# Broadcasting RMS-norm factors to all partitions by DMA through a scratch row instead of by TensorE, in a two-layer decoder trunk

## The chip, the cores and the metric

One of the eight cores of one Trainium2 chip. The metric is the device time of one execution in microseconds (us); a kernel's time is the median of its runs.

## The reference, cut to what matters

The reference is a decoder trunk of two layers over 256 tokens with D_MODEL = 1024, in float32. Each layer is a half-step SwiGLU FFN (1024 to 2816 and back), a token mixer with memory cross-attention beside it, and a second half-step FFN. Layer 0 mixes with an mLSTM, layer 1 with sliding-window attention. Ahead of each of these blocks, and once for the 256 memory tokens, stands an RMS norm:

```python
def rms_norm(x, g):
    xf = x.astype(jnp.float32)
    y = xf * lax.rsqrt(jnp.mean(xf * xf, axis=-1, keepdims=True) + EPS)
    return (y * g.astype(jnp.float32)).astype(x.dtype)
def swiglu(x, w_in, w_out):
    gate, up = jnp.split(x @ w_in, 2, axis=-1)
    return (jax.nn.silu(gate) * up) @ w_out
...
x = x + 0.5 * swiglu(rms_norm(x, ffn1_norm_g[i]), ffn1_w_in[i], ffn1_w_out[i])
hn = rms_norm(x, mix_norm_g[i])
...
x = x + 0.5 * swiglu(rms_norm(x, ffn2_norm_g[i]), ffn2_w_in[i], ffn2_w_out[i])
```

There are seven such norms: one of the memory tokens, and six of x (three per layer). The factor `rsqrt(...)` is one number per token.

## The kernel before, in words

**Layout.** Activations are kept transposed: 128 features on the partitions, 256 tokens (T) along the free axis, eight such chunks. A projection of the kind "columns" has a weight tile as TensorE's stationary operand and activations as the moving one, 128x256 per matmul; a projection of the kind "rows" has the activations stationary and 256 weight columns moving.

**Precision.** Each float32 weight tile (128 x 4 x 256) arrives by a DMA on SyncE's queue (`wtile`, L216-219) and is split by `split` (L206-214) into a high half, cast by ScalarE (L211, tile `wh`), and a rest, subtracted by VectorE (L212, tile `wl`). A product is three matmuls (`mm3`, L224-228): high by high on L225, L226 and L227 for the cross terms. There are eight buffers for each half, and five for the raw tiles.

**Norms.** The norm is not applied to x. `Norm.put` (L269-279) multiplies a finished chunk of x by the gain and splits it into `xh` and `xl`, which the next block's matmuls use at once; the squares are summed over the chunks into `acc`. The factor per token is applied to what the matmuls give. `Norm.chain` (L293-310) makes it. Two float32 matmuls (L296, recorded on the helper's line L231) with 128 tokens of `acc` as stationary operand and a column of ones as moving one give the sum over the 128 partitions, one column per half of the tokens; `rsqrt_cols` (L248-251) makes the factors `rc` (128 tokens x 2 halves) on VectorE (L250) and POOL (L251). `rc` has tokens on partitions, which is what "rows" projections need. "Columns" projections need the factor along the free axis, the same on every partition. So `bcast_rows` (L253-255) has two more float32 matmuls, with a column of `rc`, broadcast to 128 columns, as stationary operand and the identity (tile `con`) as moving one; ScalarE copies their result from PSUM to `rb` (L306) and, times 0.5, to `hrb` (L309). Five norms do the second step; the memory norm and the norm before the second mixer have `rows=False` and stop at `rc`, and the norm before the first mixer makes no `hrb`.

**Users of the row.** In an FFN `hidden` (L473-483) multiplies the gate half by `rb` (VectorE, L476), applies SiLU, multiplies by the other half (L479) and splits the result (L245, L246). `hrb` is used at the FFN's end (L544). The first mixer uses `rb` on L658, L696, L697, L754 and L757.

**Order.** TensorE's and SyncE's instructions are issued in an order written out by hand: `Weave` (L61-95) steps one main program and a set of side chains, by a clock of its own that each matmul advances, and by waiting times in `LAT` (L53). `norm=7.5` is the time from the end of a block to `chain`, `norm_b=4.8` the time from there to the broadcast; `x0_b=7.5` is the same for the first norm. A consumer waits until `ready` says that the chain has run (L502, L668). The other engines' order is set by the tile framework's scheduler. A matmul's result lies in one of eight PSUM banks (`mo`, L150).

**Lines to know.** L231: all float32 helper matmuls; L236: transposes, four of 128x128 in a row; L211, L212: weight splits; L225 to L227: the weight matmuls; L183: a mask's load on POOL's queue.

Of the kernel before, what the change touches and what calls it, by code (L numbers as in the profile page):

```python
# [10 lines left out]
F32 = mybir.dt.float32  # L11
# [3 lines left out]
AF = mybir.ActivationFunctionType  # L15
ALU = mybir.AluOpType
# [3 lines left out]
P = 128  # L20
T = 256
D = 1024
# [10 lines left out]
def constants():  # L33
# [16 lines left out]

LAT = dict(pieces=1, norm=7.5, norm_b=4.8, mnorm=2.4, x0=16.0, x0_b=7.5, mkeys=7.2, cross=9.5, cross_s=1.5,  # L53
           cross_m=3.7, cross_p=8.7, cross_o=3.0, gates=20.0, scores=2.2, scores_m=8.4, num=6.9, num_r=7.5,
           keys=5.5, keys_d=7.2, query=9.0, head=1.5, head_m=2.5, head_p=9.3, head_o=4.0)

# [42 lines left out]
def tile_trunk(ctx: ExitStack, tc: tile.TileContext, a, out):  # L99
    nc = tc.nc  # L100
    seq = [0]

    def mk(pool, shape, dt, tag):
        seq[0] += 1
        return pool.tile(shape, dt, tag=tag, name=f"{tag}_{seq[0]}")

    def pool(name, bufs, **kw):
        return ctx.enter_context(tc.tile_pool(name=name, bufs=bufs, **kw))
# [13 lines left out]
    sp = pool("sp", 2)  # L122
# [8 lines left out]
    def act(*args, **kw):  # L131
        ins = nc.scalar.activation(*args, **kw)  # L132
        if args[2] not in (AF.Copy, AF.Square):
            tabled[0] = ins
# [12 lines left out]
    def col():  # L147
        return mk(cp, [P, 16], F32, "col")

    def mo():  # L150
        return mk(pb8, [P, 512], F32, "bank")
# [15 lines left out]
    ident = con[:, C_ID:C_ID + P]  # L167
    maskd = con[:, C_MASK:C_MASK + T]
    ones = mk(cst, [P, 1], F32, "ones")
# [33 lines left out]
    pieces = [1]  # L203
# [26 lines left out]
    def mmf(ps, lhsT, rhs, n, start=True, stop=True):  # L230
        nc.tensor.matmul(ps, lhsT, rhs, start=start, stop=stop, skip_group_check=True)  # L231
        wv.now += max(0.213, n * 0.00182)
# [15 lines left out]
    def rsqrt_cols(dst, src, n, scale):  # L248
        c = col()
        nc.vector.tensor_scalar(c[:, :n], src, scale, EPS, op0=ALU.mult, op1=ALU.add)  # L250
        nc.gpsimd.tensor_tensor(out=dst, in0=c[:, :n], in1=mhalf[:, :n], op=ALU.pow)  # L251

    def bcast_rows(ps, cols):  # L253
        for h in range(2):
            mmf(ps[:, h * P:(h + 1) * P], cols[:, h:h + 1].to_broadcast([P, P]), ident, P)

    def pair(x):
        return x.unsqueeze(1).to_broadcast([P, 2, T])


    class Norm:
# [30 lines left out]

        def chain(self, gap=LAT['norm_b']):  # L293
            pc = mo()
            for h in range(2):
                mmf(pc[:, h:h + 1], self.acc[:, 0, h * P:(h + 1) * P], ones, 1)  # L296
            self.rc = mk(sp, [P, 2], F32, "rc")
            rsqrt_cols(self.rc, pc[:, 0:2], 2, 1.0 / D)
            if not self.rows:
                self.done = True  # L300
                return
            yield gap
            ps = mo()
            bcast_rows(ps, self.rc)
            self.rb = mk(sp, [P, T], F32, "rb")
            nc.scalar.copy(self.rb, ps[:, :T])  # L306
            if self.half:
                self.hrb = mk(sp, [P, T], F32, "hrb")
                act(self.hrb, ps[:, :T], AF.Copy, scale=0.5)  # L309
            self.done = True  # L310

        def ready(self):
# [55 lines left out]
    def head_norm(dst, src, n, hsc):  # L368

        hd = src.shape[2] // n  # L370
        sq, v, u = tmp(), col(), col()
        sqv = sq[:, :, :n * hd]
        act(sqv, src, AF.Square)
        nc.vector.tensor_reduce(out=v[:, 0:2 * n].rearrange("p (h m) -> p h m", h=2),
                                in_=sqv.rearrange("p h (m d) -> p h m d", m=n), axis=AX.X, op=ALU.add)
        for h in range(2):
            nc.vector.tensor_scalar(u[:, n * h:n * h + n], v[:, n * h:n * h + n], hsc[:, h:h + 1], EPS,
                                    op0=ALU.mult, op1=ALU.add)
        nc.gpsimd.tensor_tensor(out=u[:, 8:8 + 2 * n], in0=u[:, 0:2 * n], in1=mhalf[:, 0:2 * n], op=ALU.pow)  # L379
        for h in range(2):  # L380
            nc.vector.tensor_scalar(v[:, 8 + n * h:8 + n * h + n], u[:, 8 + n * h:8 + n * h + n],
                                    hsc[:, 2 + h:3 + h], None, op0=ALU.mult)
        tt(out=dst.rearrange("p h (m d) -> p h m d", m=n), in0=src.rearrange("p h (m d) -> p h m d", m=n),  # L383
           in1=v[:, 8:8 + 2 * n].rearrange("p (h m) -> p h m", h=2).unsqueeze(3).to_broadcast([P, 2, n, hd]),
           op=ALU.mult)
# [12 lines left out]
    x0 = Norm(G_F1)  # L398

    def memory():  # L400
# [22 lines left out]
        def keys(gi, kr):  # L423
            nc.scalar.copy(kT[gi], turn(kr))
            return
            yield

        for gi in range(2):
# [13 lines left out]
            norm.fold()  # L442
            wv.spawn(norm.chain(), LAT['mnorm'])
            gv = Group(wkv, 512, mh, ml, rows=True)
# [5 lines left out]
            for i, q in enumerate((first, gr)):  # L450
                kr = tmp()
                head_norm(kr, q.ps, 2, hsc)
                wv.spawn(keys(i, kr), LAT['mkeys'] + 1.5 * i)
        for gi in range(2):
# [7 lines left out]
            if gi == 0:  # L462
                with tc.issue_after(last[0].ins):
                    for c2 in range(4):
                        x0.put(xT[c2])
                wv.spawn(x0.chain(LAT['x0_b']), LAT['x0'])

# [41 lines left out]
    def ffn(x, w_in, w_out, nxt=None, mid=None):  # L509
# [13 lines left out]
        for c2 in range(4):  # L523
# [25 lines left out]
            else:  # L549
                nxt.put(xn)  # L550
        wv.spawn(nxt.chain(), LAT['norm'])

# [15 lines left out]
    def cross_spawn(gr, gi, layer, hsc, ys):  # L568
# [4 lines left out]
        def queries():  # L573
# [4 lines left out]
            for m in range(2):  # L578
                wv.spawn(head(m), LAT['cross_s'] + LAT['cross_m'] * m)
            return  # L580
            yield

        def head(m):
            hd, qT = gi * 2 + m, cell[0]
            hi, lo = ys.tiles(4 + gi)
            s = mo()
            for h in range(2):
                mmf(s[:, h * T:(h + 1) * T], qT[:, m, h * P:(h + 1) * P], kT[gi][:, m], T)
            sv = halves(s)
            c = col()  # L590
            nc.vector.tensor_reduce(out=c[:, 2:4], in_=sv, axis=AX.X, op=ALU.max, negate=True)  # L591
            p = unit(F32)
            for h in range(2):
                act(p[:, h], sv[:, h], AF.Exp, bias=c[:, 2 + h:3 + h], accum_out=c[:, 4 + h:5 + h])
            nc.vector.reciprocal(c[:, 6:8], c[:, 4:6])
            tt(out=p, in0=p, in1=c[:, 6:8].unsqueeze(2).to_broadcast([P, 2, T]), op=ALU.mult)
            yield LAT['cross_p']
            tps = mo()
            for mc in range(2):
                for h in range(2):  # L600
                    transpose(tps[:, mc * T + h * P:mc * T + (h + 1) * P], p[:, h, mc * P:(mc + 1) * P])
            pT = tmp()
            nc.scalar.copy(pT, halves(tps))
            yield LAT['cross_o']
            o = mo()
            for mc in range(2):
                mmf(o[:, :T], vM[:, mc, hd * P:(hd + 1) * P], pT[:, mc], T, mc == 0, mc == 1)
            split_plain(o[:, :T], hi[:, m], lo[:, m])
            ys.done.add(8 + hd)
# [417 lines left out]
```

## Time and profile before

| What | Value |
|---|---|
| median of 3 runs (lowest, highest) | 1012.1 us (1011.96, 1012.36) |
| the profiled execution | 1012.23 us, with a span of 1010.4 us |
| mean granted TensorE clock | 1.0 |
| HBM read, written | 180.32 MB, 1.05 MB |
| DMA over the span | mean 181 GB/s |

Reading it: times are us from the span's start unless marked ns. PE is TensorE's matmuls, PEld its weight loads (they overlap the matmuls), DVE VectorE, ACT ScalarE, POOL GpSimd, SP SyncE; a q behind an engine's name is its sequencer. A row of a group gives line, engine, operation, output<-inputs with shapes, count, busy time, mean ns of one, idle time before them, and what ended it. A row of waits gives engine, tile and line that waited, what it waited for, the total, the count and the longest. A row of the timeline begins with its start and its duration. A row of a stretch gives the stretch, its length, the busy time and count of each engine in it (PE, PEld, DVE, ACT, POOL), the granted clock, the share of the DMA engines, and GB/s. A row of one tile gives durations as min/median/max ns, and first and last start. A row of a DMA gives queue, count, size and the median time from issue to landing. Matmuls are pipelined: one of 128x256 lasts about 0.28 us in the records, while the next begins well before it ends, so the pace is read from starts.

### The profile page before, as it was taken

To read this page: it belongs to the slowest core of one execution; us is meant where nothing else is said; L and a number is where in the kernel's file an instruction comes from. 1 tells how busy PE (TensorE), PEld (TensorE's weight loads), DVE (VectorE), ACT (ScalarE), POOL (GpSimd) and SP (SyncE) were. 2 spreads that over 40 slices of the span, in tenths; PEclk is the share of its full clock that TensorE was granted. 3 is DMA by queue.
4 is the path that set the end of the run, shared out by engine and by line. 5 is a ranking of instruction groups with operands and counts; after the bars stand their busy time and mean duration, and the time that the engine had idled before them with its cause. 6 is when DMAs were issued, how large, how long until landed. Compare 5 with 4: busy or idle time off the path is not lost.

```text
span 1010.4 us, 20624 instructions
## 1 busy us (share of the span) xinstructions
PE 998.5 (99%) x8594; PEld 980.2 (97%) x8594; DVE 655.5 (65%) x1063; ACT 519.5 (51%) x764; POOL 35.7 (4%) x32
## 2 busy tenths in 40 slices
PE   8999999999999999999999999999999999999998
PEld 7999999999999999999999999999987899999998
DVE  6866665577856676665558666656787766666551
ACT  7754445446656554444445544544557754454440
POOL 1200000000001000000000000000121000000000
PEclk9999999999999999999999999999999999999999
DMA  9776656666644566665676666567541347666550
GB/s 308 242 245 200 192 180 185 199 183 179 184 139 133 167 210 195 200 189 170 192 206 205 189 191 201 173 197 198 182 131 66 100 131 220 198 189 185 188 170 21
DMA packets 173204, 182.70 MB, mean 181 GB/s; under 512 B 7124, under 2 KB 168328, under 8 KB 173112
## 3 DMA queue, kind: packets, MB, share of 16 engines
q1 hardware_dynamic: 171872, 179.60, 58.3%
q10 hardware_dynamic: 1016, 1.58, 0.5%
q8 instruction: 67, 1.10, 0.5%
q0 software_dynamic: 224, 0.22, 0.2%
q14 instruction: 25, 0.20, 0.1%
HBM read 180.32 MB, written 1.05 MB: 180 GB/s over the span
## 4 chain that ended last, share of the span: by engine, by line
PE 94%; DVE 3%; ACT 1%; DMA 1%; POOL 0%; issue 0%; SPq 0%; ACTq 0%
PE bank L225 30%; PE bank L226 30%; PE bank L227 30%; PE bank L231 2%; PE bank L236 1%; ACT u L132 1%; DVE wl L212 1%; DMA wr<-in_mem_w_kv_dram 1%; PE bank L961 1%; POOL col L379 0%; DVE col L930 0%; DVE u L383 0%; DVE col L591 0%; PE bank L925 0%; DVE u L946 0%
## 5 line engine op out<-in xcount | busy, mean ns | idle before, releaser
L212 DVE TENSOR_TENSOR wl<-wr,wh 128x1024 fp32r<-128x1024 f32 (+1 forms) x347 | 414.7, 1196 | 279.8 <-ACT wh L211 279.0
L211 ACT CAST wh<-wr 128x1024 fp32r<-128x1024 f32 (+1 forms) x347 | 356.8, 1031 | 393.1 <-PE bank L226 368.9
L225 PE MATMUL bank<-xh,wh 128*128 128x256 f32 x1544 | 429.1, 278 | 0.0
L226 PE MATMUL bank<-xl,wh 128*128 128x256 f32 x1544 | 426.8, 276 | 0.0
L227 PE MATMUL bank<-xh,wl 128*128 128x256 f32 x1544 | 426.8, 276 | 0.0
L226 PEld LDWEIGHTS bank<-xl,wh 128*128 128x128 f32 x1544 | 290.3, 188 | 0.1
L225 PEld LDWEIGHTS bank<-xh,wh 128*128 128x128 f32 x1544 | 290.0, 188 | 0.1
L227 PEld LDWEIGHTS bank<-xh,wl 128*128 128x128 f32 x1544 | 289.9, 188 | 0.0
L225 PE MATMUL bank<-u,wh 128*128 128x256 f32 x896 | 249.3, 278 | 0.0
L226 PE MATMUL bank<-u,wh 128*128 128x256 f32 x896 | 247.6, 276 | 0.0
L227 PE MATMUL bank<-u,wl 128*128 128x256 f32 x896 | 247.6, 276 | 0.0
L225 PEld LDWEIGHTS bank<-u,wh 128*128 128x128 f32 x896 | 168.2, 188 | 1.9 <-issue 1.7
L226 PEld LDWEIGHTS bank<-u,wh 128*128 128x128 f32 x896 | 168.4, 188 | 0.1
L227 PEld LDWEIGHTS bank<-u,wl 128*128 128x128 f32 x896 | 168.3, 188 | 0.0
L225 PE MATMUL bank<-wh,xh 128*128 128x256 f32 x208 | 59.7, 287 | 0.0
L226 PE MATMUL bank<-wl,xh 128*128 128x256 f32 x208 | 57.9, 278 | 0.0
L227 PE MATMUL bank<-wh,xl 128*128 128x256 f32 x208 | 57.9, 278 | 0.0
L476 DVE TENSOR_TENSOR t<-bank,rb 128x256 f32<-128x256 f32 x88 | 36.6, 420 | 7.3 <-PE bank L227 7.3
L225 PEld LDWEIGHTS bank<-wh,xh 128*128 128x128 f32 x208 | 39.1, 188 | 0.5 <-issue 0.3
L226 PEld LDWEIGHTS bank<-wl,xh 128*128 128x128 f32 x208 | 39.1, 188 | 0.1
L227 PEld LDWEIGHTS bank<-wh,xl 128*128 128x128 f32 x208 | 39.0, 187 | 0.0
L479 DVE TENSOR_TENSOR t<-t,bank 128x256 f32<-128x256 f32 x88 | 32.7, 412 | 1.8 <-ACT t L132 1.8
(171 smaller groups left out, 657.5 us busy)
## 6 DMA issues: line engine op xcount, KB each, us to landing
wr<-in_ffn_w_in_dram SPq DMA_DIRECT2D x176, 512.0 KB, 3.6
wr<-in_ffn_w_out_dram SPq DMA_DIRECT2D x80, 512.0 KB, 3.5
wr<-in_a_w_in_dram SPq DMA_DIRECT2D x28, 512.0 KB, 3.9
wr<-in_b_w_in_dram SPq DMA_DIRECT2D x14, 512.0 KB, 4.6
wr<-in_a_w_out_dram SPq DMA_DIRECT2D x12, 512.0 KB, 3.3
wr<-in_b_w_out_dram SPq DMA_DIRECT2D x12, 512.0 KB, 3.4
wr<-in_ffn_w_out_dram SPq DMA_DIRECT2D x16, 256.0 KB, 2.8
wr<-in_mem_w_kv_dram SPq DMA_DIRECT2D x7, 512.0 KB, 8.0
```

The lines of the kernel that those rows point to most:

```text
L132: ins = nc.scalar.activation(*args, **kw)
L211: last[0] = nc.scalar.copy(hi[:, i * n:(i + 1) * n], src[:, i * n:(i + 1) * n])
L212: tt(out=lo[:, i * n:(i + 1) * n], in0=src[:, i * n:(i + 1) * n], in1=hi[:, i * n:(i + 1) * n].bitcast(F32), op=ALU.subtract)
L225: nc.tensor.matmul(ps, wh, xh, start=start, stop=False, skip_group_check=True)
L226: nc.tensor.matmul(ps, wh, xl, start=False, stop=False, skip_group_check=True)
L227: nc.tensor.matmul(ps, wl, xh, start=False, stop=stop, skip_group_check=True)
L231: nc.tensor.matmul(ps, lhsT, rhs, start=start, stop=stop, skip_group_check=True)
L236: nc.tensor.transpose(ps, src, ident[:k, :k])
L476: tt(out=t[:, m], in0=ps[m][:, :T], in1=x.rb, op=ALU.mult)
L479: tt(out=t[:, m], in0=t[:, m], in1=ps[m][:, T:], op=ALU.mult)
L961: nc.tensor.matmul(o[es[e], cs], vr[:, i, js], pTs[e][:, src], start=i == 0, stop=i == 1, skip_group_check=True)
```

## The change

The two broadcast matmuls and the copies from PSUM go. In their place the factors `rc` are written as one row of 256 numbers to a scratch tensor in DRAM, and that row is read back to all 128 partitions; both DMAs are issued on POOL's queue, right behind the POOL operation that makes `rc`. `hrb` is now made from `rb` by VectorE. The sum over partitions has 128 columns of ones as moving operand (a broadcast of the one column), so that its result stands 128 times, and one column of it is read. `LAT` gives the chain 12.0 (11.0 for the first norm) between that point and `done`. Each of the five norms has a row of its own in the scratch tensor `rd`.

```diff
-LAT = dict(pieces=1, norm=7.5, norm_b=4.8, mnorm=2.4, x0=16.0, x0_b=7.5, mkeys=7.2, cross=9.5, cross_s=1.5,
+LAT = dict(pieces=1, norm=7.5, norm_b=12.0, mnorm=2.4, x0=16.0, x0_b=11.0, mkeys=7.2, cross=9.5, cross_s=1.5,
...
-    def bcast_rows(ps, cols):
-        for h in range(2):
-            mmf(ps[:, h * P:(h + 1) * P], cols[:, h:h + 1].to_broadcast([P, P]), ident, P)
-
     def pair(x):
         return x.unsqueeze(1).to_broadcast([P, 2, T])
+
+    turned = []
...
         def chain(self, gap=LAT['norm_b']):
             pc = mo()
             for h in range(2):
-                mmf(pc[:, h:h + 1], self.acc[:, 0, h * P:(h + 1) * P], ones, 1)
+                mmf(pc[:, h * P:(h + 1) * P], self.acc[:, 0, h * P:(h + 1) * P], ones.to_broadcast([P, P]), P)
             self.rc = mk(sp, [P, 2], F32, "rc")
-            rsqrt_cols(self.rc, pc[:, 0:2], 2, 1.0 / D)
+            rsqrt_cols(self.rc, pc[:, :T].rearrange("p (h t) -> p h t", h=2)[:, :, 0], 2, 1.0 / D)
             if not self.rows:
                 self.done = True
                 return
+
+            rd = a["rd"][len(turned)]
+            turned.append(self)
+            self.rb = mk(sp, [P, T], F32, "rb")
+            nc.gpsimd.dma_start(rd.rearrange("(h p) -> p h", p=P), self.rc)
+            nc.gpsimd.dma_start(self.rb, rd.partition_broadcast(P))
             yield gap
-            ps = mo()
-            bcast_rows(ps, self.rc)
-            self.rb = mk(sp, [P, T], F32, "rb")
-            nc.scalar.copy(self.rb, ps[:, :T])
             if self.half:
                 self.hrb = mk(sp, [P, T], F32, "hrb")
-                act(self.hrb, ps[:, :T], AF.Copy, scale=0.5)
+                nc.vector.tensor_scalar(self.hrb, self.rb, 0.5, None, op0=ALU.mult)
             self.done = True
...
+    aps["rd"] = nc.dram_tensor("rd_dram", (5, T), F32, kind="Internal").ap()
```

## The prediction

> **What bounds the kernel now.** I read the page first: span, the engines' busy shares, the chain of work that ended last, and the group of the weight splits. Then the groups of waits of TensorE, the order of time around the seven norms, and a table of stretches for the pace of the matmuls.
>
> ```profile
> span 1010.4 us, 20624 instructions
> PE 998.5 (99%) x8594; PEld 980.2 (97%) x8594; DVE 655.5 (65%) x1063; ACT 519.5 (51%) x764; POOL 35.7 (4%) x32
> PE 94%; DVE 3%; ACT 1%; DMA 1%; POOL 0%; issue 0%; SPq 0%; ACTq 0%
> L211 ACT CAST wh<-wr 128x1024 fp32r<-128x1024 f32 (+1 forms) x347 | 356.8, 1031 | 393.1 <-PE bank L226 368.9
> PE bank L231 <- ACT u L132: 1.5, 1, 1.5
> ...
> PE bank L920 <- ACT t L954: 0.2, 1, 0.2
> ```
>
> TensorE is busy all the time and 94% of the chain is matmuls. Its list of waits (here first and last of nine) has no wait on a norm factor: L231 waits for work of the attention heads only. And ScalarE, which makes the high halves of the weights, stands idle 368.9 us because TensorE has not yet freed a buffer. So the weight pipeline is full: eight split tiles, one in use. **Only what changes TensorE's own stream, or empties that pipeline, moves the end.** The compared instruction streams say what changes there: TensorE's and SyncE's order stay, but for five broadcast blocks that go and seven sum-of-squares blocks that become wider.
>
> Now the norm of the first FFN-to-mixer step on TensorE, in order of time:
>
> ```profile
> 223.69 0.28 PE L227 MATMUL bank<-xh,wl 128*128 128x256 f32 x1
> 223.81 0.50 PE L231 MATMUL bank<-ones,acc 128*128 128x1 f32 x4
> 224.17 0.36 PE L225 MATMUL bank<-xh,wh 128*128 128x256 f32 x1
> 224.37 0.28 PE L226 MATMUL bank<-xl,wh 128*128 128x256 f32 x1
> ...
> 229.79 0.28 PE L227 MATMUL bank<-xh,wl 128*128 128x256 f32 x1
> 229.91 0.61 PE L231 MATMUL bank<-con,rc 128*128 128x128 f32 x4
> 230.27 0.37 PE L225 MATMUL bank<-xh,wh 128*128 128x256 f32 x1
> 230.47 0.28 PE L226 MATMUL bank<-xl,wh 128*128 128x256 f32 x1
> ```
>
> And the pace, by stretches cut from one matmul's start to another's (the count of weight loads, less one, is the number of steps):
>
> ```profile
> 46.34:54.70 8.36, 8.36 (x72) 8.36 (x72) 5.90 (x6) 4.20 (x4) 2.31 (x2) 1.00 0.98 318
> 55.27:223.80 168.53, 168.53 (x1489) 168.53 (x1488) 108.65 (x143) 83.26 (x102) 0.00 (x0) 1.00 0.64 192
> 230.47:252.12 21.65, 21.65 (x193) 21.65 (x192) 16.11 (x27) 13.88 (x20) 1.91 (x1) 1.00 0.63 174
> 364.42:538.38 173.96, 173.96 (x1537) 173.96 (x1536) 110.74 (x141) 84.78 (x102) 0.00 (x0) 1.00 0.64 194
> 538.96:544.48 5.52, 5.52 (x48) 5.52 (x48) 4.72 (x22) 1.77 (x3) 0.70 (x1) 1.00 0.65 190
> 545.06:719.03 173.97, 173.97 (x1537) 173.97 (x1536) 111.03 (x146) 86.16 (x104) 0.00 (x0) 1.00 0.64 193
> 840.56:1006.37 165.81, 165.81 (x1465) 165.78 (x1463) 93.21 (x119) 68.92 (x80) 0.00 (x0) 1.00 0.54 166
> ```
>
> This is the part that the averages hide. **The same matmuls run at two paces.** From 545.06 on a step is 173.97 / 1535 = 113.3 ns; from 538.96, just before, it is 5.52 / 47 = 117.4 ns, and from 46.34 it is 8.36 / 71 = 117.7 ns. The granted clock is 1.00 in all, and the DMA traffic is 190 against 193 GB/s in the neighbouring pair, so neither explains it. What lies between is a block of TensorE: the pace turns slow at each one-column sum of squares and turns fast again at each broadcast block, five times of five, and then stays for up to 1536 matmuls. I take 4.4 ns as the difference.
>
> **The change part by part.** *Broadcast blocks out.* From the L227 at 229.79 to the L226 at 230.47 are 0.68 us, where two steps would be 0.23: a block costs 0.45 us. Five go: -2.25 us. Nothing late takes their place on TensorE, because nobody there waited for them.
>
> *Sum of squares, 128 columns for one.* The 128x1 block costs, from 223.69 to 224.37, the same 0.68 us. The broadcast block has the form that the new one will have.
>
> ```profile
> L231 PEld LDWEIGHTS bank<-con,rc x20: 187/190/192, 54.6 to 840.2; 128*128 128x128 f32 x20
> L231 PE MATMUL bank<-con,rc x20: 272/275/275, 54.7 to 840.3; 128*128 128x128 f32 x20
> L231 PE MATMUL bank<-ones,acc x28: 164/250/250, 24.6 to 834.1; 128*128 128x1 f32 x28
> ```
>
> Each record goes with a weight load of 190 ns, whatever its columns, so both blocks are paced by loads: seven widened blocks cost 0 to 0.01 us each, under 0.1 us together. The Trainium skill, "TensorE: Matmul & The Clock Gate", section "Back-to-back issue gap", gives a warm step of about 60 cycles up to 64 columns and 134 at 128; by it the 28 records would cost 28 x 74 cycles, an estimate of 0.9 us, and the sum would shrink by that. The two blocks of 0.68 us speak against it here.
>
> *The slow stretch.* With a one-column block it lasts until the broadcast block: 72 matmuls once, 48 in each of the other four norms. If the widened block leaves TensorE as the equally shaped broadcast block does, these 264 run at 113.3: -264 x 4.4 ns = -1.16 us. That is the choice in this forecast. For it: five of five broadcast blocks end fast. They were entered slow, the new one is entered fast; blocks that were entered fast and have four 128-column fp32 records too are the transposes before 38.88, 315.72 and 789.06:
>
> ```profile
> 39.09:45.67 6.58, 6.58 (x61) 6.58 (x59) 6.58 (x9) 5.93 (x9) 0.00 (x0) 1.00 0.90 283
> 316.40:321.16 4.76, 4.76 (x44) 4.76 (x43) 3.02 (x8) 3.42 (x5) 0.70 (x1) 1.00 0.36 110
> 789.27:791.77 2.50, 2.50 (x25) 2.50 (x23) 1.50 (x9) 2.50 (x10) 0.00 (x0) 1.00 0.00 0
> 729.94:732.53 2.59, 2.59 (x24) 2.59 (x23) 2.56 (x6) 1.74 (x2) 0.58 (x1) 1.00 0.48 130
> ```
>
> 113.4, 113.3 and 113.6 ns a step: all fast. The last row is the counterexample: after four transposes at 729.38 it is 2.59 / 22 = 117.7, but there the activations are the stationary operand and the pace was slow before. For that reason I book nothing for the memory norm and for the norm before the second mixer.
>
> *The factor by two DMAs.* Adds, in five norms, a write of 1 KB and a read of 128 rows on POOL's queue, with POOL waiting for the first before it issues the second, and a copy for the half on VectorE; it takes two copies off ScalarE. The nearest rows, on the same queue:
>
> ```profile
> u<-in_mask_dram POOLq DMA_DIRECT2D x1, 192.0 KB, 5.5
> sink<-in_b_sinks_dram POOLq DMA_DIRECT2D x1, 8.0 KB, 5.4
> posi<-in_positions_dram POOLq DMA_DIRECT2D x1, 1.0 KB, 5.7
> con<-in_con_dram SPq DMA_DIRECT2D x1, 196.0 KB, 8.4
> 49.34 1.75 POOL L251 TENSOR_TENSOR rc<-col,mhalf 128x2 f32<-128x2 f32 x1 [13.11 <-DVE col L250]
> 51.04 0.61 POOL L183 DMA_DIRECT2D u<-in_mask_dram  x1
> 53.51 1.23 DVE L212 TENSOR_TENSOR wl<-wr,wh 128x1024 fp32r<-128x1024 f32 x1 [0.95 <-ACT wh L211]
> 57.01 1.50 DVE L476 TENSOR_TENSOR t<-bank,rb 128x256 f32<-128x256 f32 x4
> ```
>
> The write has posi's 256 elements of 4 bytes, the read is a broadcast like sink: 5.7 + 5.4 = 11.1 us. In the tightest place, the first FFN, the factors are ready at 51.09, so the row lands at 62.2. VectorE's new order puts the half copy and the first two L476 ahead of the split that ran at 53.51; VectorE then stands still some 9 us, and that split ends near 62.2 + 0.4 + 0.75 + 1.23 = 64.6 rather than 54.74. Its tile is needed six full tiles later, 6 x 24 x 113.3 ns = 16.3 us, at 71.0. So 6.4 us of cover are left, and the wait costs nothing; at con's 8.4 us per DMA the split would end at 70.3, still in time. The mask load moves behind the two DMAs on POOL; the copies off ScalarE and onto VectorE lie on engines with idle time. All of this: 0 (bounds 0 to +1).
>
> *Start-up.* VectorE's order changes by one instruction near 26 us, where a split is just late.
>
> ```profile
> PEld bank L226 <- DVE wl L212: 1.3, 2, 1.1
> ```
>
> Of these two waits the second (0.2) goes, as its split moves ahead of two small operations: -0.1, bounds -0.2 to +0.2.
>
> **Sum**: -2.25 + 0.05 - 1.16 - 0.1 = -3.5 us. The profiled execution took 1012.23 us (span 1010.4 and 1.8 around it), the median of the runs is 0.13 lower: 1012.1 - 3.5 = **1008.6**. Its own range is 1007.8 to 1009.6.
>
> **The rivals.** *Slower: the slow pace stays.* If the widened block leaves TensorE as the one-column block does (all seven of those end slow), no broadcast block follows to reset it. The stretches from 55.27, 230.47, 364.42, 545.06 and 840.56 (the second ends where projections with stationary activations begin, which run slow anyway) hold 1488 + 192 + 1536 + 1536 + 1463 = 6215 loads; at 4.4 ns that is +27.3 us, less 2.25: **1037**. It decides early: one FFN alone is 1536 x 4.4 = 6.8 us and gives 1012.1 - 3.5 + 6.8 = 1015.4. For it: same stationary operand, same entry; against it: the shape, and that every block of 128 columns in this orientation ended fast. 13%.
>
> *Slower: the row comes too late.* If the two DMAs take over 17.5 us together in the first FFN (11.1 + 6.4), TensorE waits for the split, microsecond for microsecond; at 12 us each, 1008.6 + 6.5 = 1015. The Trainium skill, "SBUF — State Buffer", section "SBUF: two separate sides", speaks for this rival: descriptors of POOL's DMAs cannot be written while VectorE holds the shared port, and it tells of 620 ns becoming 3100. The mask load above, issued while VectorE split weights, landed in 5.5 us. 4%.
>
> *No difference.* The widened block ends slow, and the pace recovers by itself after some hundred matmuls, or the mixers' phases fall worse: the gain is the 2.25 us less 0.4 to 2: 1010.3 to 1012. 6%.
>
> **How the numbers follow.** Forecast 77%, slow pace 13%, late row 4%, no difference 6%. About 0.2% (2 us) is what a measurement of this kernel can tell from no change. Faster by more: the forecast and a little of the last case, 78%; within: 6%; slower: 16%. The range takes the forecast's own and the no-difference case: 1007.6 to 1012; the slower cases, 17%, are left out.
>
> **What would show it.** Right: the matmuls after each sum of squares step at 113.3 ns at once; the L231 rows with rc are gone; the widened block still takes 0.68 us between its neighbours; VectorE's half copy waits 5 to 10 us for the row, and no TensorE wait on a split follows. Wrong: a step of 117.7 ns that runs on through an FFN (then 1015 to 1037), or TensorE waiting for L212 near 65 to 75 us.

## The result and the profile after

| | before | after |
|---|---|---|
| median of the runs (lowest, highest) | 1012.13 us (1011.96, 1012.36) | 1042.73 us (1041.11, 1044.34) |
| the profiled execution, its span | 1012.23 us, 1010.4 us | 1043.04 us, 1041.0 us |

The ratio is 1.0302, 95% interval [1.0284, 1.032]: 3% slower, where 0.35% faster was forecast. First the page of the kernel after:

```profile
span 1041.0 us, 20586 instructions
PE 1024.9 (98%) x8574; PEld 1006.5 (97%) x8574; DVE 651.7 (63%) x1067; ACT 515.2 (49%) x755; POOL 41.3 (4%) x42
PE 86%; DVE 6%; DMA 2%; POOL 2%; issue 2%; ACT 2%; SPq 0%; DVEq 0%; ACTq 0%; POOLq 0%
L211 ACT CAST wh<-wr 128x1024 fp32r<-128x1024 f32 (+1 forms) x347 | 354.3, 1027 | 362.4 <-PE bank L226 338.4
```

TensorE has 20 matmul records fewer and is busy 26.4 us longer: most of the loss is *inside* its stream, and not in waits. ScalarE still stands idle 338.4 us for a buffer that TensorE has not freed, so the weight pipeline stayed full. The same in order of time, at the norm before the first mixer:

```profile
231.43 0.28 PE L227 MATMUL bank<-xh,wl 128*128 128x256 f32 x1
231.55 0.61 PE L231 MATMUL bank<-ones,acc 128*128 128x128 f32 x4
231.91 0.36 PE L225 MATMUL bank<-xh,wh 128*128 128x256 f32 x1
232.12 0.28 PE L226 MATMUL bank<-xl,wh 128*128 128x256 f32 x1
```

From 231.43 to 232.12 are 0.69 us, against 0.68 before: the widened block itself costs nothing. What it leaves behind does. These are the stretches after each of the five row norms, cut from the second matmul behind the block to the last before the next break (count of loads less one gives the steps, as in the prediction):

```profile
47.93:231.43 183.50, 183.50 (x1560) 183.50 (x1559) 113.99 (x150) 86.87 (x104) 2.57 (x4) 1.00 0.63 193
232.12:265.80 33.68, 33.68 (x289) 33.68 (x287) 18.37 (x30) 15.65 (x21) 3.45 (x4) 1.00 0.67 157
370.26:556.58 186.32, 186.32 (x1584) 186.32 (x1583) 113.08 (x146) 85.89 (x102) 2.94 (x3) 1.00 0.62 192
557.27:743.59 186.32, 186.32 (x1584) 186.32 (x1583) 115.52 (x173) 87.27 (x105) 2.02 (x3) 1.00 0.63 187
858.99:1036.83 177.84, 177.84 (x1512) 177.84 (x1511) 95.52 (x124) 70.05 (x80) 2.98 (x3) 1.00 0.52 165
```

186.32 / 1582 = 117.8 ns a step, in all five, at a granted clock of 1.00: **the slow pace of the prediction now lasts through every FFN.** Before, 6215 of these steps ran at 113.3 ns; at 4.44 ns each that is +27.6 us.

The second loss is in the first mixer. Waits of the kernel after (engine, tile and line that waited, for what, total, count, longest):

```profile
DVE hrb L309 <- DMA rb<-rd_dram: 47.2, 4, 12.8
...
DVE u L658 <- DMA rb<-rd_dram: 10.2, 1, 10.2
...
PE bank L236 <- DVE u L383: 2.4, 1, 2.4
...
PE bank L226 <- DVE wl L212: 0.9, 1, 0.9
```

In the four FFNs VectorE waits for the row for 11.8 us each, and TensorE does not feel it: its only wait on a split (0.9 us) is at the start. In the first mixer VectorE waits 10.2 us in L658 and is then late with a head norm (L383), for which TensorE waits 2.4 us (the kernel before has no such wait on L236); two smaller waits and slower work around them follow. The row's own way there, on GpSimd, and the two DMAs over the kernel (KB each, median us from issue to landing):

```profile
232.51 0.72 POOL L251 TENSOR_TENSOR rc<-col,mhalf 128x2 f32<-128x2 f32 x1 [169.04 <-DVE col L250]
233.53 0.75 POOL L304 DMA_DIRECT2D rd_dram<-rc  x1 [0.30 <-POOL rc L251]
242.19 0.56 POOL L305 DMA_DIRECT2D rb<-rd_dram  x1 [7.92 <-DMA rd_dram<-rc]
```

```profile
rb<-rd_dram POOLq DMA_DIRECT2D x5, 128.0 KB, 3.6
rd_dram<-rc POOLq DMA_DIRECT2D x5, 1.0 KB, 9.4
```

The third is at the start. The same stretch, before and after; the third number from the end is the granted clock:

```profile
10.00:26.00 16.00, 14.77 (x121) 14.17 (x120) 13.99 (x25) 13.48 (x23) 0.66 (x1) 1.00 1.07 385
```

```profile
10.00:26.00 16.00, 14.31 (x106) 13.71 (x106) 13.49 (x23) 12.73 (x22) 0.00 (x0) 0.89 1.07 385
```

TensorE got 0.89 of its clock there, and 15 matmuls from 14.68 on took 214 ns each: +1.6 us, and a difference that comes and goes. The one of the four runs after with a mean clock of 1.00 took 1041.11 us, and among the experiments some profiles show it and others not, with and without the change's DMAs.

Followed along the span by equal instructions, the profiled difference of 30.6 us is: pace +27.6, five broadcast blocks gone -2.25, first mixer +3.8 (2.4 of it the wait above), start +1.6, rest -0.1.

### The profile page after: what moved, and what is told of

Same layout as the page of the kernel before. It is cut to its first block, busy times and chain, and to the rows that moved or that the text cites. A ratio compares the mean times of both kernels' runs of the same rounds, so it can differ in the third digit from the quotient of the medians.

```text
span 1041.0 us, 20586 instructions
## 1 busy us (share of the span) xinstructions
PE 1024.9 (98%) x8574; PEld 1006.5 (97%) x8574; DVE 651.7 (63%) x1067; ACT 515.2 (49%) x755; POOL 41.3 (4%) x42
## 4 chain that ended last, share of the span: by engine, by line
PE 86%; DVE 6%; DMA 2%; POOL 2%; issue 2%; ACT 2%; SPq 0%; DVEq 0%; ACTq 0%; POOLq 0%
PE bank L225 28%; PE bank L227 28%; PE bank L226 28%; DVE wl L212 2%; POOL col L379 2%; PE bank L231 2%; ACT u L132 1%; PE bank L236 1%; DMA rd_dram<-rc 1%; DMA wr<-in_mem_w_kv_dram 1%; PE bank L961 1%; DMA rb<-rd_dram 1%; DVE col L374 0%; DVE col L591 0%; DVE u L383 0%
## 5 line engine op out<-in xcount | busy, mean ns | idle before, releaser
L211 ACT CAST wh<-wr 128x1024 fp32r<-128x1024 f32 (+1 forms) x347 | 354.3, 1027 | 362.4 <-PE bank L226 338.4
L225 PE MATMUL bank<-xh,wh 128*128 128x256 f32 x1544 | 435.2, 282 | 0.0
L226 PE MATMUL bank<-xl,wh 128*128 128x256 f32 x1544 | 433.4, 281 | 0.0
L227 PE MATMUL bank<-xh,wl 128*128 128x256 f32 x1544 | 433.4, 281 | 0.0
L226 PEld LDWEIGHTS bank<-xl,wh 128*128 128x128 f32 x1544 | 294.3, 191 | 0.1
L227 PEld LDWEIGHTS bank<-xh,wl 128*128 128x128 f32 x1544 | 291.5, 189 | 0.0
L225 PE MATMUL bank<-u,wh 128*128 128x256 f32 x896 | 252.8, 282 | 0.0
L226 PE MATMUL bank<-u,wh 128*128 128x256 f32 x896 | 251.1, 280 | 0.0
L227 PE MATMUL bank<-u,wl 128*128 128x256 f32 x896 | 251.1, 280 | 0.0
L226 PEld LDWEIGHTS bank<-u,wh 128*128 128x128 f32 x896 | 170.6, 190 | 0.1
L227 PEld LDWEIGHTS bank<-u,wl 128*128 128x128 f32 x896 | 169.0, 189 | 0.0
L226 PE MATMUL bank<-wl,xh 128*128 128x256 f32 x208 | 58.1, 279 | 0.0
L227 PE MATMUL bank<-wh,xl 128*128 128x256 f32 x208 | 58.1, 279 | 0.0
L132 ACT ACTIVATE t<-t 128x512 f32<-128x512 f32 x44 | 27.7, 629 | 55.4 <-DVE t L476 55.4
L226 PEld LDWEIGHTS bank<-wl,xh 128*128 128x128 f32 x208 | 39.1, 188 | 0.1
L227 PEld LDWEIGHTS bank<-wh,xl 128*128 128x128 f32 x208 | 39.0, 187 | 0.0
```

The costliest lines, as they stand in the source:

```text
L211: last[0] = nc.scalar.copy(hi[:, i * n:(i + 1) * n], src[:, i * n:(i + 1) * n])
L225: nc.tensor.matmul(ps, wh, xh, start=start, stop=False, skip_group_check=True)
L226: nc.tensor.matmul(ps, wh, xl, start=False, stop=False, skip_group_check=True)
L227: nc.tensor.matmul(ps, wl, xh, start=False, stop=stop, skip_group_check=True)
```

## The experiments

"Kept broadcasts" and the like below are names for the runs. Times are medians; the ratio is to the kernel before on the same chip, over all runs of both, so it is not exactly the quotient of two medians. Square brackets hold its 95% interval.

### One part at a time

**Dense ones.** The kernel after, but the moving operand of the sums is a real 128x128 tile of ones and not one column with a zero step.

```diff
+    ones_sq = mk(cst, [P, P], F32, "ones_sq")
+    nc.vector.memset(ones_sq, 1.0)
-  mmf(pc[:, h * P:(h + 1) * P], self.acc[...], ones.to_broadcast([P, P]), P)
+  mmf(pc[:, h * P:(h + 1) * P], self.acc[...], ones_sq, P)
```

> Changed kernel, with the moving operand of the widened sums read from a real 128x128 tile of ones instead of one column repeated by a zero step. Theory A (the pace of the weight matmuls is set by the last float32 block, and any block with the squares as stationary operand ends slow): steps of 117.8 ns through every FFN, 1042.7 us. Theory B (the zero step of the moving operand is what makes the block end slow): 113.3 ns after every sum, so 6215 + 264 steps less 4.45 ns each, 1042.7 - 27.6 - 1.2 = 1013.9 us. Theory C (the pace does not matter, late rows and stalls make the 30 us): 1042.7.

Measured: 1035.53 us, 1.0225 [1.0207, 1.0243], between the expectations, so none of the theories stands. The stretches, cut as above:

```profile
46.44:229.93 183.49, 183.49 (x1560) 183.49 (x1559) 113.99 (x150) 86.96 (x104) 2.57 (x4) 1.00 0.67 193
230.62:252.00 21.38, 21.38 (x191) 21.38 (x190) 7.41 (x11) 6.99 (x9) 2.02 (x3) 1.00 0.66 120
369.93:556.25 186.32, 186.32 (x1584) 186.32 (x1583) 113.08 (x146) 85.89 (x102) 2.94 (x3) 1.00 0.64 192
556.94:736.24 179.30, 179.30 (x1584) 179.30 (x1583) 115.31 (x173) 87.62 (x105) 2.03 (x3) 1.00 0.66 193
851.56:1029.41 177.85, 177.85 (x1513) 177.85 (x1511) 95.53 (x124) 70.06 (x80) 2.98 (x3) 1.00 0.55 166
```

Slow, fast (21.38 / 189 = 113.1), slow, fast (179.30 / 1582 = 113.3), slow. The two that end fast are those that were *entered* slow; the other three were entered fast. The block acts as a switch. That is the new theory: the pace that a block leaves depends on the pace it meets and on its operands.

**DMA with one column.** The kernel after with the old one-column sums (`mmf(pc[:, h:h + 1], ..., ones, 1)`).

> Changed kernel, with the sums of squares back at one column; the DMAs stay. Theory A: the width is irrelevant, the block ends slow either way and no broadcast block resets it: 1042.7 us within 2. Theory B: slow here as well, since the one-column block ends slow in the kernel before: 1042.7. If the widening itself costs something: 1041 or less.

Measured: 1042.58 us, 1.0284 [1.0256, 1.0313], all FFNs at 117.8 ns in the profile. Width has nothing to do with it; the missing broadcast block has. (One of four runs took 1037.23, 5 us less than the others; it was not profiled, so this stays open.)

**Wide only.** The kernel before with the 128-column sums alone.

> Kernel before, with the widened sums alone; broadcast by TensorE stays. Theory A: 72 and four times 48 slow steps as before, reset by each broadcast block: 1012.1 us within 0.5. If widening costs by its columns: 28 records of 31 ns more, 1013.0. If a block's end depended on the pace at which it is entered, the broadcast blocks would show it only when entered fast, which they are not here.

Measured: 1012.15 us, 0.9994 [0.998, 1.0008]. The broadcast block ends each slow stretch as before:

```profile
539.11:544.52 5.41, 5.41 (x48) 5.41 (x47) 4.64 (x21) 1.77 (x3) 0.70 (x1) 1.00 0.68 199
545.21:719.07 173.86, 173.86 (x1536) 173.86 (x1535) 110.90 (x146) 86.17 (x104) 0.00 (x0) 1.00 0.64 193
```

5.41 / 46 = 117.6 ns ahead of it, 173.86 / 1534 = 113.3 behind.

**Kept broadcasts.** The kernel after, its row by DMA, but with the two broadcast matmuls still issued and their result not used.

```diff
-            yield gap
+            yield 4.8
+            ps = mo()
+            for h in range(2):
+                mmf(ps[:, h * P:(h + 1) * P], self.rc[:, h:h + 1].to_broadcast([P, P]), ident, P)
+            yield gap - 4.8
```

> Changed kernel, with the two broadcast matmuls per norm kept at their old place (4.8 us of the weave's clock after the sum); nobody reads their result, the row still comes by DMA. Theory A: the broadcast block resets the pace: 1042.7 - 27.6 + 2.25 = 1017.3 us, and what is left above 1012.1 is the DMAs' own cost (waits of TensorE in the first mixer 3.8 us, start-up 1.6). Theory C (late rows make the loss): above 1038.

Measured: 1017.82 us (1015.74 to 1018.4), 1.0046 [1.0031, 1.0062]. Some 25 us come back by issuing matmuls that nobody reads. The profiled execution took 1015.74 us, 3.5 over the kernel before, and that is the first mixer: from its sum to the next norm's sum are 137.69 us against 133.94, and TensorE waits there as in the kernel after. The other three runs took 1.7 to 2.7 us more, at mean granted clocks of 0.997 and 0.998 against 1.00.

```profile
PE bank L236 <- DVE u L387: 2.4, 1, 2.4
```

### Is it a switch?

**Broadcast twice.** The kernel before, each broadcast block issued again some 24 matmuls later: the second copy meets the fast pace.

```diff
             bcast_rows(ps, self.rc)
...
+            yield 2.6
+            bcast_rows(mo(), self.rc)
```

> The kernel before with each of the five broadcast blocks issued a second time about 24 matmuls behind the first, so that the second is entered at the fast pace (its result is not used). Theory T (toggle): a block with a dense moving operand that is entered fast ends slow, so the FFNs behind it run at 117.8 ns: 1012.1 + 2.25 (five more blocks of 0.45) + 27.6 = about 1042. Rival R2: a broadcast block always leaves the fast pace: 1012.1 + 2.25 = 1014.4.

Measured: 1041.27 us, 1.0286 [1.0271, 1.0301]. One norm, in three stretches (behind the sum, behind the first broadcast, behind the second):

```profile
366.21:371.62 5.41, 5.41 (x47) 5.41 (x47) 3.10 (x4) 1.67 (x2) 1.54 (x1) 1.00 0.93 290
372.31:374.81 2.50, 2.50 (x24) 2.50 (x23) 1.86 (x3) 1.16 (x3) 0.00 (x0) 1.00 0.76 252
375.49:553.33 177.84, 177.84 (x1512) 177.84 (x1511) 108.89 (x138) 82.90 (x99) 0.00 (x0) 1.00 0.60 186
```

117.6, then 2.50 / 22 = 113.6, then 177.84 / 1510 = 117.8 ns. The same instructions turn the pace fast when they meet slow, and slow when they meet fast, five times of five. This run changes nothing else in the kernel, has no DMA of the row, and loses the whole 27 us.

**One-pass sums, broadcasts as before.** The kernel before with only the sums as matmuls of the FFNs' type.

```diff
+    nc.scalar.copy(onesr, ones.to_broadcast([P, P]))
-  tt(out=self.acc[:, 0], in0=self.acc[:, 0], in1=self.acc[:, 1], op=ALU.add)
+  self.accr = mk(ap1, [P, T], F32R, "accr")
+  tt(out=self.accr, in0=self.acc[:, 0], in1=self.acc[:, 1], op=ALU.add)
-  mmf(pc[:, h:h + 1], self.acc[...], ones, 1)
+  mmf(pc[:, h * P:(h + 1) * P], self.accr[:, h * P:(h + 1) * P], onesr, P)
```

> The kernel before, broadcasts on TensorE as they were, with only the sums of squares as one-pass matmuls (fp32r, a dense 128x128 tile of ones; the summed squares are rounded to that type, so outputs differ a little). The sum blocks then leave the pace fast, and the float32 broadcast block is entered fast. Theory T (toggle): it ends slow, and the cheaper sums make the kernel slower: 1012.1 - 1.2 (264 steps before the broadcasts now fast) - 1.5 (seven sum blocks of 0.23 instead of 0.45) + 27.6 = about 1037. Rival R2: a broadcast block always leaves the fast pace: 1012.1 - 1.2 - 1.5 = about 1009.4.

Measured: 1038.62 us, 1.0262 [1.0247, 1.0277]. Behind the sum, then behind the broadcast, at the third row norm:

```profile
365.97:371.19 5.22, 5.22 (x48) 5.22 (x47) 3.34 (x4) 1.90 (x2) 1.55 (x1) 1.00 0.97 297
371.86:552.53 180.67, 180.67 (x1536) 180.67 (x1535) 110.76 (x141) 84.70 (x102) 0.00 (x0) 1.00 0.62 188
```

113.5, then 117.8 ns. A cheaper, shorter sum makes the kernel 26 us slower, because the broadcast block is now entered fast, and ends slow five times of five.

**Broadcast of three and of four matmuls.** The kernel before with the block's first matmul issued twice (`mmf(ps[:, 0:P], self.rc[:, 0:1]..., ident, P)` ahead of `bcast_rows`), and with the whole block issued twice in a row (a second `bcast_rows(ps, self.rc)`).

> The kernel before with the first broadcast matmul of each block issued twice (three float32 matmuls instead of two, the same result), entered slow. Theory W: they end fast: 1012.1 + 1.1 = about 1013.2. Theory L: another end than with two in some or all of the five: up to 1041.

> The kernel before with each broadcast block computed twice with nothing between (four float32 matmuls instead of two, the same result). The blocks are entered slow, behind the one-column sums. Theory W (a block acts as a whole): they end fast: 1012.1 + 2.2 (five times two matmuls of two records of 0.11) = about 1014.4. Theory L (length decides, every two matmuls toggle): they end slow, 1014.4 + 27.6 = about 1042.

Measured: three 1041.01 us, 1.0281 [1.0266, 1.0297]; four 1014.73 us, 1.0029 [1.0015, 1.0043]. The stretch behind the fourth row norm's block, of three first, of four second:

```profile
562.02:742.69 180.67, 180.67 (x1537) 180.67 (x1535) 111.08 (x145) 85.72 (x104) 0.00 (x0) 1.00 0.62 186
```

```profile
548.39:722.25 173.86, 173.86 (x1536) 173.86 (x1535) 110.89 (x145) 85.80 (x104) 0.00 (x0) 1.00 0.64 193
```

Entered slow, three end slow (five of five) and four end fast. So the block does not act as a whole (theory W falls with three), and it is not a switch per pair either (theory L, as stated for four, falls too). The number of matmuls in the block matters, by a rule that two, three and four do not give away. The run with four also prices the block: ten more matmuls and 2.5 us (1.5 to 4.4 by the interval), near the 2.25 us taken for those removed.

### Repairs of the pace

**Transposes after.** The kernel after with four 128-column transposes right behind each sum block.

```diff
+            if self.rows:
+                pt = mo()
+                for i in range(4):
+                    transpose(pt[:, i * P:(i + 1) * P], ident)
```

> The changed kernel with four 128-column transposes on TensorE right behind the sum block in each of the five norms along the tokens (their result is not used). Theory T: TensorE has two paces, a block of float32 matmuls decides by the pace it is entered at and by its operands which one it leaves, and a block that is dense on its moving side, entered slow, ends fast. Then the FFNs behind the norms run at 113.3 instead of 117.8 ns a matmul: 1042.7 - 27.6 (6215 steps of 4.45 ns) - 1.2 (the 264 steps between sum and broadcast, slow before as well) + 2.0 (five blocks of 0.4) = about 1016, with the waits of the first mixer still there. Rival R1: only the stationary operand of the broadcast block (one column read with a zero step) resets the pace, and transposes do not: 1042.7 + 2.0 = about 1044.7, all FFNs at 117.8.

Measured: 1019.39 us, 1.0074 [1.0054, 1.0095]; the five stretches are fast. It is 3 us over the expectation (the profiled execution, 1017.42 us, 1.4 over it), and TensorE's wait in the first mixer has grown from 2.4 to 4.6 us: with faster matmuls it arrives there sooner, and the row does not.

**One-pass sums.** The kernel after with the sums of "One-pass sums, broadcasts as before" (`accr`, `onesr`), in all seven norms.

> The changed kernel with the sums of squares of the five norms along the tokens as one-pass matmuls of the type that the FFNs use (fp32r), with a dense 128x128 tile of ones; it rounds the summed squares to that type first, so the outputs differ a little. Theory F: the float32 type of the sum block is what changes the pace. Then all FFNs stay at 113.3 ns: 1042.7 - 27.6 - 1.2 - about 1 for the cheaper blocks = about 1013, with the waits of the first mixer (3 to 4 us) in it. Rival: any matmul that breaks the row of 256-column steps changes it: about 1041 with all FFNs at 117.8, or a mix of paces as with the dense float32 ones (about 1035).

Measured: 1015.39 us, 1.0013 [0.9995, 1.0031]; all five stretches fast. The wait in the first mixer is now 5.6 us:

```profile
PE bank L238 <- DVE u L386: 5.6, 1, 5.6
```

From 258.40 on, within that wait, the granted clock was 0.50 for 6.8 us:

```profile
258.40:265.20 6.80, 3.93 (x19) 3.93 (x20) 5.03 (x11) 4.14 (x6) 2.60 (x2) 0.50 0.81 243
```

Five of the seven profiles with a TensorE wait of 2.4 us or more at this place have such a stretch, of 3.4 to 6.8 us, that begins in the wait or at most 1.4 us behind it; the kernel after and "Kept broadcasts" do not, and none of the other ten profiles has one there. So a late row can cost clock besides the wait. How much, no run here separates.

**Both one-pass.** The kernel before with sums and broadcasts as matmuls of the FFNs' type, no DMA.

> The kernel before with the sums and the broadcasts both as one-pass matmuls (fp32r; the summed squares and the factors are rounded to that type, so outputs differ a little; the broadcasts stay on TensorE and there is no DMA). Theory F: no float32 block is left around the FFNs, so the pace stays fast throughout: 1012.1 - 1.2 - 1.5 - 1.1 (five broadcast blocks of 0.23 instead of 0.45) = about 1008.3. Rival: a one-pass block with a zero step changes the pace too: about 1036.

Measured: 1017.91 us, 1.0052 [1.0037, 1.0067]: a miss of 10 us. The sums ended fast five of five, the broadcasts only three of five. Third and fourth row norm:

```profile
362.80:536.67 173.87, 173.87 (x1536) 173.87 (x1535) 110.69 (x141) 85.23 (x102) 0.00 (x0) 1.00 0.64 194
542.81:723.49 180.68, 180.68 (x1536) 180.68 (x1536) 111.48 (x149) 86.31 (x104) 0.00 (x0) 1.00 0.62 186
```

173.87 / 1534 = 113.3 and 180.68 / 1535 = 117.7. The one slow FFN and the slow mixer stretch (some 190 steps) make 7.7 of the 10 us. The profiled execution is the fastest of the four, 1015.78 us, 7.5 over the expectation, so these 7.7 us account for it; the other three, at lower mean clocks (0.996 to 0.998), were not profiled. So float32 is not needed for the change: a one-pass block can do it too, here in two cases of five.

### The late row

**DMAs unused.** The kernel before with the two DMAs added into a tile that nobody reads.

```diff
+            nc.gpsimd.dma_start(rd.rearrange("(h p) -> p h", p=P), self.rc)
+            nc.gpsimd.dma_start(rb2, rd.partition_broadcast(P))
             yield gap
```

> The kernel before with the two DMAs of the change added on GpSimd's queue and their row not used. Theory W: the DMAs cost only by the row that comes late: 1012.1 within 0.2%. Rival: their small pieces disturb the weights' transfers or GpSimd's other work: 1014 to 1016, with new waits of TensorE.

Measured: 1012.39 us, 1.0003 [0.9994, 1.0013]. As traffic the DMAs cost nothing that this run can tell (1.3 us at most, by the interval); what counts is who waits for the row.

**ScalarE's queue.** "Kept broadcasts" with `nc.scalar.dma_start` for both DMAs.

> The changed kernel with the broadcast matmuls kept (result unused), as in the run with the kept broadcasts (1017.8), and the two DMAs of the row issued by ScalarE's queue instead of GpSimd's. Theory Q: GpSimd's queue makes the write land late (10 us from issue), and ScalarE's would land in 3 to 5: the row is there before the first mixer's head norm, TensorE does not wait there, 1014 to 1015. Rival: the 256 rows of 4 bytes are slow on any queue: about 1017.8, with TensorE waiting some 3 us in the first mixer.

Measured: 1016.53 us, 1.004 [1.0024, 1.0056], and the same wait of TensorE (2.4 us). The write lands after 9.2 us, against 10.6 on GpSimd's queue in "Kept broadcasts", and in the first mixer the row is first used 14.5 us after the operation that makes `rc` begins, on either queue. Theory Q falls. And the read's wait for the write now stops ScalarE, which casts the weights:

```profile
ACT wh L211 <- DMA rd_dram<-rc: 56.4, 5, 12.3
```

**Write of 8 bytes.** "Kept broadcasts" with the scratch row written as pairs, `rd.rearrange("(p h) -> p h", p=P)`. The row then holds the factors in another order than its users read them, so the run is for the timing alone.

> The changed kernel with the broadcast matmuls kept (result unused), as in the run with the kept broadcasts (1017.8), and the write of the row as 128 pieces of 8 bytes instead of 256 of 4; the row then has its factors in the wrong order. Theory P: the write's 10 us are its pieces, at half of them it lands in 5 to 6, the row is there 5 us earlier, and the waits of the first mixer (3.3 us) go: about 1014.5. Rival: the write takes 9 to 10 us whatever its pieces: 1017.8.

Measured: 1013.29 us, 1.0013 [1.0004, 1.0023]. TensorE's wait of 2.4 us is gone (its longest on a head norm is 0.7 us, as in the kernel before), and the DMAs show why:

```profile
rb<-rd_dram POOLq DMA_DIRECT2D x5, 128.0 KB, 4.1
rd_dram<-rc POOLq DMA_DIRECT2D x5, 1.0 KB, 6.3
```

The same 1 KB in 128 pieces lands in 6.3 us, in 256 pieces in 10.6. The pieces are those of the access pattern in the edit. On GpSimd's queue the two traces record equally many packets (624), so they do not show what became of the pieces, and two shapes do not give a price per piece.

### Both terms taken away

**Pairs and one-pass sums.** The kernel after with one-pass sums, whose stationary operand takes every second token, so that the row is written as pairs in the right order; the norm before the first mixer has a second sum block for its factors in columns.

```diff
+            byt = self.accr.rearrange("p (t h) -> p h t", h=2)
+            for h in range(2):
+                mmf(pc[:, h * P:(h + 1) * P], byt[:, h], onesr, P)
...
-            nc.gpsimd.dma_start(rd.rearrange("(h p) -> p h", p=P), self.rc)
+            nc.gpsimd.dma_start(rd.rearrange("(p h) -> p h", p=P), rct)
```

> The changed kernel, DMAs and all, with the sums as one-pass matmuls (the summed squares rounded to fp32r, so outputs differ a little) and with the token order of the row norms' sums turned to pairs, so that the row is written as 128 pieces of 8 bytes in the right order; the first mixer's norm, which needs the factors in columns too, has a second sum block for them. Both failed terms are taken away: against the run with one-pass sums alone (1015.4, of which 5.6 TensorE's wait in the first mixer) that wait goes and one block of 0.23 comes: about 1010, some 0.2% below the kernel before. Rival: a strided stationary operand or the second block changes the pace, or the row is late all the same: 1015 or more.

Measured: 1010.76 us (1009.0 to 1012.12), 0.9977 [0.9964, 0.9991]: below the kernel before by 0.1 to 0.4%. The third and fourth row norm's stretches, and the DMAs:

```profile
359.01:538.32 179.31, 179.31 (x1584) 179.31 (x1584) 113.29 (x146) 86.31 (x102) 2.75 (x3) 1.00 0.66 199
538.79:718.10 179.31, 179.31 (x1584) 179.31 (x1583) 115.75 (x173) 87.92 (x105) 1.84 (x3) 1.00 0.65 194
```

```profile
rb<-rd_dram POOLq DMA_DIRECT2D x5, 128.0 KB, 4.0
rd_dram<-rct POOLq DMA_DIRECT2D x5, 1.0 KB, 6.1
```

113.3 ns right behind the sums, and TensorE's longest wait on a head norm is 0.8 us, against 0.7 before. The profiled execution took 1010.43 us, of which 1.7 are the start (the first row norm's sum begins at 47.48 us instead of 45.78, with a granted clock of 0.89 from 10 to 26 us). Without that it lies near the forecast of 1008.6, though its one-pass sums are also some 0.8 us cheaper (six blocks at 0.46 instead of 0.68 us, one pair at 1.16). So what else the change may have hidden is about 1 us, an estimate.

### What the blocks did, all runs together

Counts are of the five row norms' blocks in the profiles, by the pace at which they were entered.

| block | entered fast, ends | entered slow, ends |
|---|---|---|
| two float32, moving one column of ones or its zero step | slow 3 of 3 (after) | slow 2 of 2 (after) |
| two float32, moving dense ones | slow 3 of 3 | fast 2 of 2 |
| two float32, moving the dense identity (broadcast) | slow 10 of 10 | fast 10 of 10 (before, broadcast twice) |
| three, four of the last | | slow 5 of 5, fast 5 of 5 |
| two one-pass, moving dense ones | fast 13 of 13 (both runs of one-pass sums, both one-pass) | fast 2 of 2 (one-pass sums, broadcasts as before) |
| two one-pass, broadcast | fast 3, slow 2 | |

Two things on record say that the entry and the operands alone do not fix the outcome. First, the pace also changes where there is no block. In the kernel before, projections with stationary activations run from 241.25 to 252.01. Where stationary weights come back, the pace turns slow from one matmul to the next:

```profile
252.01 0.28 PE L227 MATMUL bank<-wh,xl 128*128 128x256 f32 x1
252.13 0.28 PE L225 MATMUL bank<-xh,wh 128*128 128x256 f32 x1
```

```profile
252.13:257.78 5.65, 5.65 (x50) 5.65 (x49) 4.61 (x11) 2.59 (x3) 1.91 (x1) 1.00 0.97 278
```

That is 5.65 / 48 = 117.7 ns, behind 21.65 / 191 = 113.4 in the prediction's stretch from 230.47 to 252.12. Over the 17 profiles this place was entered fast eleven times and left slow each time; entered slow six times, it was left fast three times and slow three times. Second, at the two norms that are not in the table, where the activations are stationary, the blocks of "One-pass sums" were entered fast and ended slow, both times (113.3, then 117.7 ns).

The table is what the runs show for the row norms. What in TensorE makes two stable paces of the same loads and matmuls, and why these blocks move it as they do, no run here shows.

## Why the prediction was wrong, step by step

**The bound: right.** TensorE's stream still sets the end, and the FFNs' weight pipeline stayed full.

**Broadcast blocks out, -2.25: right.** They are gone, and doubling them cost 2.5 us; in that trace a block with its neighbours, from the L227 at 366.18 to the L226 at 367.31, takes 1.13 us where one of two matmuls takes 0.68.

**Sums of 128 columns, about 0: right.** "Wide only" lies at 0.9994 [0.998, 1.0008], and the block takes 0.69 us with its neighbours. The Trainium skill, "TensorE: Matmul & The Clock Gate", section "Back-to-back issue gap", would have it cost an estimated 0.9 us by figures that it gives for an isolated matmul; the interval ends at 0.8 above, so the run speaks against using them in this stream.

**The slow stretch, -1.16: this is the step that failed, and it has +27.6 in its place.** The choice was that "the widened block leaves TensorE as the equally shaped broadcast block does". It does not. Three things went wrong in it. The five broadcast blocks were evidence for a block that is *entered slow*; the prediction said so, and took them for evidence all the same. Entered fast, the very same block ends slow ("Broadcast twice", "One-pass sums, broadcasts as before"). Its stand-in for "entered fast", the transposes, is another kind of block: four instructions of one record each, where the sum is two of two records. And the widened block has a zero step on its moving side, which the broadcast block has on its stationary side; with dense ones it would have acted as the broadcast block acts, and still have ended slow three times of five. The rival that the slow pace stays had the mechanism, its 6215 steps and its step of 4.4 ns right. One reading in it was wrong, at no cost: projections with stationary activations do not "run slow anyway". Before the change they ran at the fast pace inside its second stretch, up to 252.01, and the slow pace began behind them. Why the widened block leaves the slow pace, in terms of TensorE's workings, stays open.

**The two DMAs, 0: mis-sized, +3.8.** The estimate was 5.7 + 5.4 = 11.1 us. The read was faster (3.6), the write slower (9.4), and with GpSimd's issue the row lands 13 to 17 us after `rc`. In the FFNs the cover held, as worked out there: VectorE waited 11.8 us where some 9 were expected, and TensorE did not. In the first mixer it was not looked for: the prediction called the first FFN "the tightest place" and never followed L658 to the head norm. The rival of the late row had the right mechanism at the wrong place and price. The Trainium skill, "SBUF — State Buffer", section "SBUF: two separate sides", was cited there: VectorE holding the shared port delays GpSimd's descriptors. That cannot be the main reason for the slow write here: on ScalarE's queue it took 9.2 us too, and on GpSimd's with half the pieces 6.3.

**Start-up, -0.1:** the granted clock (0.89 against 1.00) hides any such gain; +1.6 in this profile, not in others.

The rival of 1037 and the measured 1042.7 differ by the mixer and the start: 1037 + 3.8 + 1.6 = 1042.4. The two slower rivals held 13% and 4%, so 17% together; the 16% beside "slower" is a slip of one.

## What to carry to other kernels

Read the pace of equal matmuls stretch by stretch, and when a small block sits at a change of it, treat the block as part of the timing: before removing or altering it, ask at which pace it is entered, and take as evidence only blocks of the same length, the same operands' strides and the same entry. Where a pace can last 1500 steps, the odds of that one step decide the forecast, and the range must reach to it. Do not price a small DMA by its bytes alone, since here the shape of the pieces moved it by 4 us, and work out its cover for every consumer, not for the first.

## What the runs showed of the hardware that was not expected

- The same stream of loads and 128x256 matmuls holds one of two paces, 113.3 or 117.8 ns, for up to 1582 steps at an equal granted clock; two unused matmuls per norm moved a whole kernel by 29 us (1012 to 1041).
- A block of two float32 matmuls with a dense moving operand switched the pace both ways; entered slow, three left it slow and four left it fast. At a change from stationary activations to stationary weights the pace switched with no block between.
- A write of 1 KB to DRAM took 9.2 to 10.6 us as 256 pieces of 4 bytes on either queue, and 6.1 to 6.3 us as 128 pieces of 8.
- While a read issued from ScalarE's queue waited for the write before it, ScalarE did no other work: 56.4 us over five norms.
- In five of seven profiles the granted clock fell to 0.50 for 3.4 to 6.8 us in a TensorE wait of 2.4 to 5.6 us or shortly behind it.
